# A two-block float32 transformer on one core: PSUM banks planned with the order of the products, eleven direct pairs turned into seven-product pairs, one weight sum made by an adding transfer, and a longer split ending

## The chip, the cores and the metric

One core of one Trainium2 chip runs the kernel. The metric is device microseconds of one execution, lower is better. Durations in the text come from one profiled execution of the kernel; its matmuls start one after the other and overlap in the pipeline, so the cost of one is the distance between starts, not its printed length.

## The reference

Two models run one after the other on a sequence of 512 tokens with 1024 features. The first has two layers of attention, retention, pooling and a convolutional MLP. The second puts 16 learned tokens ahead (528 tokens) and has two layers of gated MLP, mixer, gated MLP. The change touches only the second model's four gated MLPs and its end:

```python
def swiglu(x, w_gate, w_up, w_down):
    return (jax.nn.silu(x @ w_gate) * (x @ w_up)) @ w_down

for l in range(DEPTH):                                   # DEPTH = 2
    h = h + 0.5 * swiglu(rmsnorm(h, g[l, 0]), gate[l, 0], up[l, 0], down[l, 0])
    h = h + mixer(rmsnorm(h, g[l, 1]), ...)
    h = h + 0.5 * swiglu(rmsnorm(h, g[l, 2]), gate[l, 1], up[l, 1], down[l, 1])
return rmsnorm(h, final_norm)[:, 16:]
```

The width inside the MLP is 2816, so gate and up have 22 column blocks of 128 each. The last of the four MLPs needs only the 512 real tokens; the other three work on 528.

## The kernel before, in words

Activations lie transposed in SBUF: eight tiles `xt` of 128 features by 528 tokens. Every float32 operand is kept as a high part and a low part (`wsplit` L225, `split`, `xsplit`): ScalarE writes the rounded high part (`whi`, L226), VectorE the difference (`wlo`, L227), and TensorE adds three matmuls per block, high by high, high by low, low by high. So each weight tile of 128 x 512 costs one DMA on SP's queue, one ScalarE and one VectorE instruction.

`ffn2` (L1175) runs one gated MLP. Its 22 pairs (one block of gate, one of up) are done in three rounds that end at pairs 8, 16 and 22 (`ROUNDS`); after each round the down projection adds that round's activations into `xt`. A pair can be done in two ways:

- **direct** (`whole`, L1071): the gate block and then the up block, each with 8 k-steps of three matmuls over all tokens. With 528 tokens a matmul is cut in two (256 and 272 columns), so the pair has 96 matmuls; with 512 tokens it has 48 of 512 columns. It needs four weight parts.
- **seven products** (`strassen`, L1089): gate and up are seen as a 2 x 2 matrix of half blocks a, b (gate) and c, d (up), the tokens as two halves, and a Winograd form needs seven products instead of eight. A product has 4 k-steps of three matmuls over half the tokens, 12 matmuls, so the pair has 84. It needs seven weight parts: a, b, d and four sums of weights, made on VectorE in `parts_of` (L1031, the sums at L1049), and four sums of activations per k, made once per MLP by `form` (L340).

The names in the trace: `gu` is the PSUM tile of a direct block; `y`, `x`, `z` are those of the seven products. Y takes p1, p6, p7, p4 one on top of the other and ScalarE copies it out after each (L1104, L1113, L1121, L1126); X takes p2; Z takes p5 and p3; VectorE adds X and Z in (L1098). `act` (L1204) multiplies by the norm's factor, applies Silu, multiplies gate by up and splits.

What sets the order: `product_order` (L1136) writes the order of a round's products by hand, with a latency LAT of 24 matmuls (two products) between a product and one that needs its copy, and with three PSUM tiles to hold. TensorE keeps that order; SP's loads, the sums and the splits keep theirs (`queue`); the rest is placed by the framework's scheduler. A product's weights are split LEAD = 6 products ahead in the program; the buffers of raw, sum, high and low tiles are in `WB`. PSUM has a pool P of three tiles of two banks and a pool S of two banks; before, Y and Z come from P and X from S.

Some pairs are direct by a list, `DIRECT`: pairs 3, 12 and 18 in the first MLP, where three pairs come from work started ahead, and 0, 1, 5, 12 and 18 in the other three, where pairs 0 and 1 cover the wait for the norm's factor `rb`. At that entry (L1228 on) three blocks are multiplied before `rb` is known; then for each of the two pairs ahead the missing block is multiplied, some `form`s are made, the gate block is read out of PSUM by `mul_r` (VectorE, L447) and `act` follows. Three of the four forms of an MLP are made earlier, in `finish` (L331) of the stage ahead.

`ending` (L1281) closes the kernel: the last output block of the last down projection is done in two halves of 256 tokens, and each half has its chain: add to `xt`, square, sum (`compact`, tile `ssq`), `rsqrt` in ten small VectorE instructions, broadcast through TensorE (`bc`), eight multiplications in `finals` (L1305, tile `fy`) and eight output DMAs.

Of the kernel before, what the change touches and what calls it, by code (L numbers as in the profile page):

```python
# [49 lines left out]
WB = {1024: {"raw": 3, "whi": 5, "wlo": 5}, 512: {"raw": 6, "sum": 4, "whi": 8, "wlo": 8}}  # L50
# [11 lines left out]
class Net:  # L62
    def __init__(self, ctx, tc, d):
# [16 lines left out]
        self.forms = None  # L80
        self.pinned = False
# [135 lines left out]
    def wtile(self, n):  # L217
        dt = F32 if n in ("raw", "sum") else F32R
        return self.wp.tile([128, self.wu], dt, tag=n, name=self.nm(n), bufs=WB[self.wu][n])
# [111 lines left out]
    def finish(self, k, T, g):  # L331
# [4 lines left out]
        if self.forms is not None and NK // 2 <= k < NK - 1:  # L336
            self.form(k - NK // 2, T, g)
        return r

    def form(self, k, T, g):  # L340
# [7 lines left out]
        stt = lambda o, i, s, j: nc.vector.scalar_tensor_tensor(  # L348
            out=o, in0=i, scalar=s, in1=j, op0=ALU.mult, op1=ALU.subtract
        )  # L350
# [680 lines left out]
    def parts_of(self, gsrc, usrc):  # L1031


        nc = self.nc
        t = {}

        def get(n):
            if n in t:
                return t[n]
            if n in "abcd":  # L1040
                h = slice(512 * (n in "bd"), 512 * (n in "bd") + 512)
                t[n] = self.wtile("raw")
                self.queue("raw", nc.sync.dma_start(t[n], (gsrc if n in "ab" else usrc)[:, h]))
            else:
                i, j = {"s1": "cd", "s2": ("s1", "a"), "s3": "ac", "s4": ("b", "s2")}[n]
                i, j = get(i), get(j)
# [12 lines left out]
        return parts  # L1059
# [11 lines left out]
    def whole(self, i, xs, T, rb, act):  # L1071
# [3 lines left out]
        def one(o):  # L1075
            def go(w):
# [985 lines left out]
```

## Time and profile before

| | us |
|---|---|
| three runs, median (lowest to highest) | 3576.71 (3575.93 to 3577.52) |
| the profiled execution, its own time | 3577.7 |
| its span, first to last instruction | 3575.9 |
| TensorE busy | 3501.3 (98%), 23291 matmuls |
| VectorE busy | 2437.5 (68%) |
| ScalarE busy | 1718.5 (48%) |
| GpSimd busy | 44.3 (1%) |
| mean granted TensorE clock | 0.991 |
| DMA | 304.94 MB, mean 85 GB/s |

The four MLPs with their down projections stand at about 1236 to 1612, 2051 to 2418, 2418 to 2795 and 3205 to 3557 us of the span. A timeline row reads: start, length, engine, line, operation, output<-inputs, shape, count, and in brackets the engine's idle time ahead and what ended it.

### The profile page before, as it was taken

To read this page: it belongs to the slowest core of one execution; us is meant where nothing else is said; L and a number is where in the kernel's file an instruction comes from. 1 tells how busy PE (TensorE), PEld (TensorE's weight loads), DVE (VectorE), ACT (ScalarE), POOL (GpSimd) and SP (SyncE) were. 2 spreads that over 40 slices of the span, in tenths; PEclk is the share of its full clock that TensorE was granted. 3 is DMA by queue.
4 is the path that set the end of the run, shared out by engine and by line. 5 is a ranking of instruction groups with operands and counts; after the bars stand their busy time and mean duration, and the time that the engine had idled before them with its cause. 6 is when DMAs were issued, how large, how long until landed. Compare 5 with 4: busy or idle time off the path is not lost.

```text
span 3575.9 us, 59662 instructions
## 1 busy us (share of the span) xinstructions
PE 3501.3 (98%) x23291; PEld 3123.4 (87%) x23291; DVE 2437.5 (68%) x4715; ACT 1718.5 (48%) x3151; POOL 44.3 (1%) x184
## 2 busy tenths in 40 slices
PE   8999999999999999999999999999999999999998
PEld 6778888778888899998898999998999987788987
DVE  6778753776874387676545777678677764677767
ACT  3654432365543364354574454454444457545443
POOL 1000000000000000000000000000000000000000
PEclk9999999999999999999999999999999999999999
DMA  4213323212333232331111222332333212223232
GB/s 151 65 48 109 97 89 107 81 60 67 99 95 93 70 105 89 95 107 61 55 61 57 83 92 92 94 102 77 96 107 93 76 54 64 65 85 105 92 104 71
DMA packets 142954, 304.94 MB, mean 85 GB/s; under 512 B 16436, under 2 KB 24660, under 8 KB 142672
## 3 DMA queue, kind: packets, MB, share of 16 engines
q1 hardware_dynamic: 138672, 292.88, 26.1%
q0 software_dynamic: 2560, 6.93, 0.6%
q8 instruction: 183, 3.00, 0.3%
q10 hardware_dynamic: 1440, 1.32, 0.1%
q14 instruction: 99, 0.81, 0.1%
HBM read 298.97 MB, written 2.10 MB: 84 GB/s over the span
## 4 chain that ended last, share of the span: by engine, by line
PE 73%; DVE 5%; ACT 2%; issue 1%; DMA 0%; DVEq 0%; ACTq 0%
PE dn L241 15%; PE g L241 12%; PE y L241 11%; PE up L241 7%; PE gu L241 6%; PE z L241 5%; PE wo L241 3%; PE x L241 3%; PE pa L241 1%; PE pb L241 1%; PE oa L1531 1%; PE sc L1497 1%; DVE wlo L227 1%; PE go L1761 1%; PE ptr L1514 1%
## 5 line engine op out<-in xcount | busy, mean ns | idle before, releaser
L226 ACT ACTIVATE whi<-raw 128x512 fp32r<-128x512 f32 (+3 forms) x880 | 620.0, 708 | 879.2 <-PE dn L241 340.5
L227 DVE TENSOR_TENSOR wlo<-raw,whi 128x512 fp32r<-128x512 f32 (+3 forms) x880 | 687.8, 783 | 401.2 <-ACT whi L226 386.9
L241 PE MATMUL g<-xh,whi 128*128 128x256 f32 (+4 forms) x1192 | 330.4, 333 | 10.0 <-ACT xh L315 5.7
L241 PE MATMUL g<-xl,whi 128*128 128x256 f32 (+4 forms) x1192 | 317.9, 320 | 0.1
L241 PE MATMUL g<-xh,wlo 128*128 128x256 f32 (+4 forms) x1192 | 316.1, 320 | 0.0
L241 PE MATMUL up<-xl,whi 128*128 128x512 f32 (+1 forms) x768 | 288.7, 376 | 0.1
L241 PE MATMUL up<-xh,wlo 128*128 128x512 f32 (+1 forms) x768 | 288.6, 376 | 0.0
L241 PE MATMUL up<-xh,whi 128*128 128x512 f32 (+1 forms) x768 | 287.9, 376 | 0.0
L241 PE MATMUL dn<-fah,whi 128*128 128x256 f32 (+1 forms) x1238 | 286.4, 300 | 1.2 <-ACT fah L235 0.6
L241 PE MATMUL dn<-fah,wlo 128*128 128x256 f32 (+1 forms) x1238 | 285.3, 299 | 0.0
L241 PE MATMUL dn<-fal,whi 128*128 128x256 f32 (+1 forms) x1238 | 285.1, 299 | 0.0
L226 ACT ACTIVATE whi<-sum 128x512 fp32r<-128x512 f32 x268 | 169.2, 632 | 219.0 <-PE dn L241 72.4
L241 PEld LDWEIGHTS g<-xh,whi 128*128 128x128 f32 (+1 forms) x1192 | 198.0, 188 | 46.1 <-issue 18.1
L227 DVE TENSOR_TENSOR wlo<-sum,whi 128x512 fp32r<-128x512 f32 x268 | 184.2, 687 | 47.9 <-ACT whi L226 43.7
L241 PEld LDWEIGHTS g<-xh,wlo 128*128 128x128 f32 (+1 forms) x1192 | 200.3, 188 | 15.4
L241 PEld LDWEIGHTS g<-xl,whi 128*128 128x128 f32 (+1 forms) x1192 | 200.7, 189 | 14.1 <-issue 1.6
L241 PEld LDWEIGHTS dn<-fah,whi 128*128 128x128 f32 x1238 | 199.8, 188 | 10.8 <-ACT fah L235 3.9
L241 PEld LDWEIGHTS dn<-fal,whi 128*128 128x128 f32 x1238 | 199.4, 188 | 7.9 <-DVE fal L236 0.8
L241 PEld LDWEIGHTS dn<-fah,wlo 128*128 128x128 f32 x1238 | 199.7, 188 | 7.3
L241 PEld LDWEIGHTS up<-xl,whi 128*128 128x128 f32 x768 | 145.1, 189 | 28.3 <-DVE xl L316 0.5
L241 PEld LDWEIGHTS up<-xh,wlo 128*128 128x128 f32 x768 | 145.2, 189 | 28.0
L241 PEld LDWEIGHTS up<-xh,whi 128*128 128x128 f32 x768 | 144.7, 189 | 27.5
(503 smaller groups left out, 8704.0 us busy)
## 6 DMA issues: line engine op xcount, KB each, us to landing
raw<-w_up SPq DMA_DIRECT2D x88, 512.0 KB, 3.6
raw<-ffn_g SPq DMA_DIRECT2D x176, 256.0 KB, 2.6
raw<-ffn_u SPq DMA_DIRECT2D x176, 256.0 KB, 2.9
raw<-ffn_d SPq DMA_DIRECT2D x160, 256.0 KB, 2.7
raw<-w_in SPq DMA_DIRECT2D x136, 256.0 KB, 2.6
raw<-w_down SPq DMA_DIRECT2D x32, 512.0 KB, 3.5
raw<-w_in SPq DMA_DIRECT2D x25, 512.0 KB, 3.6
raw<-w_out SPq DMA_DIRECT2D x16, 512.0 KB, 3.5
```

The source lines that it names most:

```text
L226: h = self.nc.scalar.activation(hi[:, c], raw[:, c], AF.Copy)
L227: l = self.nc.vector.tensor_tensor(out=lo[:, c], in0=raw[:, c], in1=hi[:, c], op=ALU.subtract)
L241: i = self.nc.tensor.matmul(*a, **k)
L1497: nc.tensor.matmul(o, lhsT=q, rhs=kk[:, kc], start=i == 0, stop=i == len(ops) - 1)
L1514: nc.tensor.transpose(tr[:, 128 * b : 128 * b + 128], p[:, 128 * b : 128 * b + 128], self.ident)
L1531: nc.tensor.matmul(o[a], lhsT=lh, rhs=rh, start=b == 0, stop=b == 4)
L1761: nc.tensor.matmul(o(b), lhsT=lh, rhs=rh, start=i == 0, stop=i == len(terms) - 1)
```

## The change

Seven edits in one diff. (1) `DIRECT` loses pairs 12 and 18 in the first MLP and 5, 12 and 18 in the other three: eleven pairs by this diff become seven-product pairs. (2) `product_order` now plans the two PSUM pools by themselves and returns which pool each product takes: p1 from P or S, p2 and p5 from S or P. (3) The Winograd form is rewritten with other signs, so that all weight sums are sums: t1 = c+d, t2 = t1+a, t3 = t2+b, t4 = a+c; one product is negated in `form` and one factor in `act`. (4) t4 is not made on VectorE any more: SP loads a into a tile `acc` (two buffers) and a DMA on GpSimd's queue adds c to it. High and low weight buffers go from 8 to 7. (5) Raw loads are issued AHEAD = 5 products before their splits. (6) At the entry of the three MLPs, `act` comes before the forms, and two forms instead of three are made in the stage ahead. (7) `ending` does the last two output blocks in halves, with the second half's second PSUM tile from S; the factor is copied to SBUF, and both halves' final multiplications come after both chains in the program.

```diff
-WB = {..., 512: {"raw": 6, "sum": 4, "whi": 8, "wlo": 8}}
+WB = {..., 512: {"raw": 6, "sum": 4, "acc": 2, "whi": 7, "wlo": 7}}
 LEAD = 6
-USES = {"p1": ("a",), "p2": ("b",), "p6": ("s2",), "p5": ("s1",), "p7": ("s3",), "p4": ("d",), "p3": ("s4",), "g": "ab", "u": "cd"}
+AHEAD = 5
+USES = {"p1": ("a",), "p2": ("b",), "p6": ("t2",), "p5": ("t1",), "p7": ("t4",), "p4": ("d",), "p3": ("t3",), "g": "ab", "u": "cd"}
-DIRECT = (0, 1, 5, 12, 18), (3, 12, 18)
+DIRECT = (0, 1), (3,)
...
-        if self.forms is not None and NK // 2 <= k < NK - 1:
+        if self.forms is not None and NK // 2 <= k < NK // 2 + self.early:
...
-        nc.scalar.activation(t[:, a], x1[:, a], AF.Copy, scale=g1)
-        stt(u[:, a], x1[:, b], g1, t[:, a])
-        stt(v[:, a], x2[:, b], g2, u[:, a])
-        nc.vector.tensor_tensor(out=u[:, b], in0=v[:, a], in1=t[:, a], op=ALU.subtract)
+        nc.scalar.activation(t[:, a], x1[:, b], AF.Copy, scale=g1)
+        stt(u[:, a], x1[:, a], g1, t[:, a])
+        stt(u[:, b], x2[:, b], g2, t[:, a])
+        stt(v[:, a], x1[:, a], g1, u[:, b], ALU.add)
         stt(v[:, b], x2[:, a], g2, v[:, a])
-        self.forms.append((self.split(u[:, :T], "fu"), self.split(v[:, :T], "fv")))
+        h, l = self.slot("fvh", F32R), self.slot("fvl", F32R)
+        nc.scalar.activation(h[:, :T], v[:, :T], AF.Copy, scale=-1.0)
+        stt(l[:, :T], v[:, :T], -1.0, h[:, :T])
+        self.forms.append((self.split(u[:, :T], "fu"), (h, l)))
...
+        of = {"t1": "cd", "t2": ("t1", "a"), "t3": ("t2", "b")}
+
+        def ahead(n):
+            if n in of:
+                for x in of[n]:
+                    ahead(x)
+            elif n not in t:
+                t[n] = self.wtile("acc" if n == "t4" else "raw")
+                self.queue("raw", nc.sync.dma_start(t[n], src["a" if n == "t4" else n]))
+                if n == "t4":
+                    nc.gpsimd.dma_start(t[n], src["c"], accum_op=ALU.add)
...
-                op = ALU.add if n == "s1" else ALU.subtract
-                self.queue("sum", nc.vector.tensor_tensor(out=t[n], in0=i, in1=j, op=op))
+                self.queue("sum", nc.vector.tensor_tensor(out=t[n], in0=i, in1=j, op=ALU.add))
...
+        bank = lambda kd, n: self.P(n)[:, 0, :h] if kd == "P" else self.S(n)[:, :h]
-            Y = ps["Y"] = self.P("y")[:, 0, :h]
+            Y = ps["Y"] = bank(kd, "y")
-            X = self.S("x")[:, :h]
+            X = bank(kd, "x")
-            Z = ps["Z"] = self.P("z")[:, 0, :h]
+            Z = ps["Z"] = bank(kd, "z")
...
-        takes, frees = {"p1", "p5", "g", "u"}, {"p4", "p3", "g", "u"}
+        takes = {"p1": "PS", "p5": "SP", "p2": "SP", "g": "P", "u": "P"}
+        frees = {"p4": "p1", "p3": "p5", "p2": "p2", "g": "g", "u": "u"}
-        hold = []
+        pool, has = {"P": [0] * 3, "S": [0] * 2}, {}
...
                 if o in takes:
-                    busy = [f for f in hold if f is None or f > t]
...
+                    at, _, kd = min((max(at, min(pool[q])), j, q) for j, q in enumerate(takes[o]))
+                    if at >= inf:
+                        continue
...
-            nc.vector.tensor_tensor(out=s[:, :T], in0=s[:, :T], in1=u, op=ALU.mult)
+            if scale:
+                nc.vector.scalar_tensor_tensor(out=s[:, :T], in0=u, scalar=-1.0, in1=s[:, :T], op0=ALU.mult, op1=ALU.mult)
...
+                gt = ps[0] if o == 4 else self.mul_r(ps[0], rb, "fg")
+                if not done:
+                    act(o // 2, gt, ps[1], False)
                 forms(1 + (o == 0) - (o == 4))
-                gt = ps[0] if o == 4 else self.mul_r(ps[0], rb, "fg")
-                act(o // 2, gt, ps[1], False)
+                if done:
+                    act(o // 2, gt, ps[1], False)
...
-            for n in range(len(order) + LEAD):
-                if n < len(order):
-                    i, o = order[n]
+            for n in range(-AHEAD, len(order) + LEAD):
+                if n + AHEAD < len(order):
+                    i, o, _ = order[n + AHEAD]
                     if i not in get:
                         get[i] = self.parts_of(srcs[2 * ms[i]], srcs[2 * ms[i] + 1])
-                    w[i, o] = [get[i](p) for p in USES[o]]
+                    if o == "p7":
+                        get[i][1]("t4")
+                if 0 <= n < len(order):
+                    i, o, _ = order[n]
+                    w[i, o] = [get[i][0](p) for p in USES[o]]
...
-                self.forms = self.next_forms
+                self.forms, self.early = self.next_forms, 2
...
-                self.ending(out, self.wload(dsrc(NK - 1)), acts, rb)
+                self.ending(out, [self.wload(dsrc(i)) for i in (NK - 2, NK - 1)], acts, rb)
...
-        ps = [self.outs(1, NX, "dn")[0][0] for _ in range(2)]
+        ps = [[self.outs(1, NX, "dn")[0][0] for _ in ws], [self.outs(1, NX, "dn")[0][0], self.S("dl")]]
...
+            for m, p, w in zip((NK - 2, NK - 1), ps[hf], ws):
...
             self.bcast(self.rsqrt(pss, bl, 1), bl, bc)
-            self.finals(out, bc, c)
+            rb = self.slot("rbe")
+            nc.scalar.copy(rb[:, c], bc[:, c])
+            bcs.append((rb, c))
+        for rb, c in bcs:
+            self.finals(out, rb, c)
```

## Rows read from the trace of the kernel before

**Rows 1.** The page: busy time of TensorE, its share and instructions.

```profile
PE 3501.3 (98%) x23291; PEld 3123.4 (87%) x23291; DVE 2437.5 (68%) x4715; ACT 1718.5 (48%) x3151; POOL 44.3 (1%) x184
```

**Rows 2.** Busy time by stretch, in the third MLP: a run of products, and an entry.

```profile
core 0: us, PE busy (x) PEld busy (x) DVE busy (x) ACT busy (x) POOL busy (x), PEclk, DMA share, GB/s
2565.56:2603.56 38.00, 38.00 (x315) 38.00 (x313) 32.14 (x55) 22.71 (x45) 0.00 (x0) 1.00 0.37 119
...
2446.00:2447.40 1.40, 1.40 (x6) 1.40 (x7) 1.15 (x2) 0.63 (x2) 0.00 (x0) 0.50 0.00 0
```

**Rows 3.** Timeline of TensorE: first matmuls of stretches, with 528 and with 512 tokens.

```profile
2565.56 0.28 PE L241 MATMUL y<-xh,whi 128*128 128x264 f32 x1
...
2603.56 0.41 PE L241 MATMUL gu<-xh,whi 128*128 128x256 f32 x2
...
2609.41 0.28 PE L241 MATMUL y<-fvh,whi 128*128 128x264 f32 x1
...
3254.58 0.39 PE L241 MATMUL gu<-xh,whi 128*128 128x512 f32 x1
...
3260.12 0.28 PE L241 MATMUL y<-fuh,whi 128*128 128x256 f32 x1
...
3261.54 0.39 PE L241 MATMUL gu<-xh,whi 128*128 128x512 f32 x1
```

**Rows 4.** The page: splits of summed weights, all four MLPs.

```profile
L227 DVE TENSOR_TENSOR wlo<-sum,whi 128x512 fp32r<-128x512 f32 x268 | 184.2, 687 | 47.9 <-ACT whi L226 43.7
```

**Rows 5.** Timeline of VectorE inside that run of products.

```profile
2585.41 0.70 DVE L236 TENSOR_TENSOR fal<-fg,fah 128x528 fp32r<-128x528 f32 x1
2586.03 0.43 DVE L1098 TENSOR_TENSOR fu<-z,fu 128x264 f32<-128x264 f32 x1
...
2586.71 0.68 DVE L227 TENSOR_TENSOR wlo<-raw,whi 128x512 fp32r<-128x512 f32 x1
2587.31 0.68 DVE L227 TENSOR_TENSOR wlo<-sum,whi 128x512 fp32r<-128x512 f32 x1
```

**Rows 6.** Tile y: what TensorE sat idle for ahead of its matmuls (us, times).

```profile
  ACT fg L1104: 4.6, 4
```

**Rows 7.** Timeline of TensorE at the entry of the third MLP.

```profile
2424.34 0.48 PE L241 MATMUL gu<-xh,whi 128*128 128x256 f32 x2 [1.73 <-DVE fd L1269]
...
2431.34 0.49 PE L241 MATMUL gu<-xh,whi 128*128 128x256 f32 x2 [0.90 <-DVE fd L1269]
...
2445.99 0.78 PE L241 MATMUL gu<-xh,whi 128*128 128x256 f32 x2 [4.37 <-DVE fg L447]
...
2454.10 0.28 PE L241 MATMUL y<-xh,whi 128*128 128x264 f32 x1
```

**Rows 8.** Timeline of ScalarE and VectorE at the same entry.

```profile
2438.72 0.66 ACT L441 COPY rbc<-bc 128x512 f32<-128x512 f32 x2 [5.48 <-PE bc L418]
...
2445.15 0.70 DVE L447 TENSOR_TENSOR fg<-gu,rbc 128x528 f32<-128x528 f32 x1
```

**Rows 9.** DMA issues: count, KB each, median us from issue to landing.

```profile
raw<-ffn_g SPq DMA_DIRECT2D x176, 256.0 KB, 2.6
...
ropc<-rope_ax POOLq DMA_DIRECT2D x2, 264.0 KB, 3.2
...
sda<-rope_da POOLq DMA_DIRECT2D x2, 256.0 KB, 5.9
```

**Rows 10.** Timeline of ScalarE: first copy of Y in that run of products.

```profile
2567.68 0.36 ACT L1104 COPY fg<-y 128x264 f32<-128x264 f32 x1
```

**Rows 11.** Timeline of TensorE and VectorE after the last down projection.

```profile
3556.33 0.28 PE L241 MATMUL dn<-fah,wlo 128*128 128x256 f32 x1
...
3560.34 3.22 DVE L1310 SCALAR_TENSOR_TENSOR fy<-xt,v,bc 128x256 f32<-128x256 f32 x8 [0.81 <-PE bc L418]
3563.48 0.41 DVE L1294 SCALAR_TENSOR_TENSOR fd<-dn,rbc 128x256 f32<-128x256 f32 x1
...
3569.75 3.22 DVE L1310 SCALAR_TENSOR_TENSOR fy<-xt,v,bc 128x256 f32<-128x256 f32 x8 [1.38 <-PE bc L418]
```

More of the change, by code (lines that the diff above doesn't have):

```diff
@@ L80, in __init__ @@
         self.forms = None
+        self.early = 3
         self.pinned = False
@@ L217, in wtile @@
     def wtile(self, n):
-        dt = F32 if n in ("raw", "sum") else F32R
+        dt = F32 if n in ("raw", "sum", "acc") else F32R
         return self.wp.tile([128, self.wu], dt, tag=n, name=self.nm(n), bufs=WB[self.wu][n])
@@ L1035, in parts_of @@
         t = {}
-        def get(n):
[L1038 to L1046, printed above, removed]
+        src = {n: (gsrc if n in "ab" else usrc)[:, 512 * (n in "bd") : 512 * (n in "bd") + 512] for n in "abcd"}
+        of = {"t1": "cd", "t2": ("t1", "a"), "t3": ("t2", "b")}
[8 more added lines that the diff above has]
+                    nc.gpsimd.dma_start(t[n], src["c"], accum_op=ALU.add)
+        def get(n):
+            ahead(n)
+            if n not in t:
+                i, j = (get(x) for x in of[n])
                 t[n] = self.wtile("sum")
-                op = ALU.add if n == "s1" else ALU.subtract
-                self.queue("sum", nc.vector.tensor_tensor(out=t[n], in0=i, in1=j, op=op))
+                self.queue("sum", nc.vector.tensor_tensor(out=t[n], in0=i, in1=j, op=ALU.add))
             return t[n]
@@ L1057, in parts @@
             return h, l
-        return parts
+        return parts, ahead
     def prod(self, o, w, xs, c, first):
@@ L1150, in product_order @@
                     break
-                at = max([t] + [end[m, d] + (0 if (d, o) in (("p1", "p2"), ("p1", "p5"), ("p5", "p7")) else LAT) for d in need.get(o, ()) if (m, d) in end])
                 if any((m, d) not in end for d in need.get(o, ())):
                     continue
+                at = max([t] + [end[m, d] + (0 if (d, o) in (("p1", "p2"), ("p1", "p5"), ("p5", "p7")) else LAT) for d in need.get(o, ())])
+                kd = None
                 if o in takes:
-                    busy = [f for f in hold if f is None or f > t]
-                    if len(busy) >= 3:
-                        if None in busy and sum(f is None for f in busy) >= 3:
-                            continue
-                        at = max(at, sorted(f for f in busy if f is not None)[len(busy) - 3])
+                    at, _, kd = min((max(at, min(pool[q])), j, q) for j, q in enumerate(takes[o]))
+                    if at >= inf:
+                        continue
                 if best is None or at < best[0]:
-                    best = (at, m, o)
-            at, m, o = best
+                    best = (at, m, o, kd)
+            at, m, o, kd = best
             t = at + (48 if o in ("g", "u") else 12)
@@ L1165, in product_order @@
             left.remove((m, o))
-            if o in takes:
-                hold = [f for f in hold if f is None or f > at]
-                hold.append(t + LAT if o in ("g", "u") else None)
-            elif o in frees:
-                hold.remove(None)
-                hold.append(t + LAT)
-            out.append((m, o))
+            if kd:
+                j = pool[kd].index(min(pool[kd]))
+                pool[kd][j] = inf
+                has[m, o] = kd, j
+            if o in frees:
+                q, j = has[m, frees[o]]
+                pool[q][j] = t + LAT
+            out.append((m, o, kd))
         return out
@@ L1261, in ffn2 @@
             if fin:
-                self.forms = self.next_forms
+                self.forms, self.early = self.next_forms, 2
             dsrc = lambda i: dw[i][:, 128 * m0 : 128 * m1]
-            for i in range(NK - 1 if fin and out is not None else NK):
+            for i in range(NK - 2 if fin and out is not None else NK):
                 p = self.outs(1, T, "dn")[0]
@@ L1288, in ending @@
             bl = (2 * hf, 2 * hf + 1)
-            n = len(acts)
-            for k in range(n):
-                self.mm3(ps[hf], ws, 128 * k, acts[k], NX, k == 0, k == n - 1, halves=(hf,))
-            xv = self.xt[m][:, c]
-            t = self.slot("fd")
-            nc.vector.scalar_tensor_tensor(
-                out=t[:, c], in0=ps[hf][:, c], scalar=0.5, in1=rf[:, c], op0=ALU.mult, op1=ALU.mult
-            )
-            nc.vector.tensor_tensor(out=xv, in0=t[:, c], in1=xv, op=ALU.add)
-            self.sumsq(m, xv, c)
+            for m, p, w in zip((NK - 2, NK - 1), ps[hf], ws):
+                for k in range(n):
+                    self.mm3(p, w, 128 * k, acts[k], NX, k == 0, k == n - 1, halves=(hf,))
+                xv = self.xt[m][:, c]
+                t = self.slot("fd")
+                nc.vector.scalar_tensor_tensor(
+                    out=t[:, c], in0=p[:, c], scalar=0.5, in1=rf[:, c], op0=ALU.mult, op1=ALU.mult
+                )
+                nc.vector.tensor_tensor(out=xv, in0=t[:, c], in1=xv, op=ALU.add)
+                self.sumsq(m, xv, c)
             pss = self.S("ssq")
```

32 lines of the change are left out of this document (18 added, 14 removed).

## The prediction, made before the changed kernel was run

> **What bounds the kernel.** I read the page first: TensorE is busy 98% of the span [rows 1], so a saving counts only if it takes matmuls off TensorE or ends one of its few waits. Next the busy time by stretch: in a run of 26 products TensorE is busy 38.00 of 38.00 us at full granted clock, VectorE 32.14 and ScalarE 22.71, GpSimd nothing [rows 2]. So the MLPs are bound by TensorE, VectorE is the next in line, and GpSimd's queue is free. Then the timeline for the pace of each kind of work [rows 3], and last the places where TensorE sits idle [rows 6, 7] and the tail, where it has nothing left to do [rows 11].
>
> **Eleven direct pairs become seven products.** By the diff the lists lose 2 pairs in the first MLP and 3 in each of the other three: 8 with 528 tokens, 3 with 512 (I count eleven). With 528 tokens the 26 products from 2565.56 to 2603.56 take 38.00 us, 1.462 each, and the half of a direct pair that follows takes 2609.41 - 2603.56 = 5.85 [rows 3]. A pair costs 2 x 5.85 = 11.70 direct and 7 x 1.462 = 10.23 in products: 1.47 saved. With 512 tokens a half takes 5.54 and a product 1.42 [rows 3]: 11.08 against 9.94, 1.14 saved. Sum: 8 x 1.47 + 3 x 1.14 = **15.2 us**, all on the path, since TensorE has no gap there.
>
> **Does VectorE keep up?** The 268 splits of sums are four for each of 67 pairs [rows 4]. On VectorE a split or a sum of 512 columns takes 0.60 from start to start, a pass over all tokens 0.62, over half of them 0.34 [rows 5]. Per pair before: 7 splits, 4 sums, 3 halves and 3 whole passes, 11 x 0.60 + 3 x 0.34 + 3 x 0.62 = 9.5 us beside 10.23 of TensorE (93%). Without the fourth sum: 8.9 (87%). So the relief by the direct pairs is not needed any more: a round of only products asks less of VectorE per microsecond than a stretch of products does now, and that runs without a gap [rows 2]. Three splits more on ScalarE for each pair, and the negation (other signs and a product in one pass of the same kind), cost nothing: ScalarE is 60% busy there [rows 2].
>
> **The adding transfer.** It replaces a sum by an SP load of a, then a GpSimd DMA that waits for it and adds c; the trace has no adding DMA. Bounds: the load 2.6 us, GpSimd's plain loads between 3.2 and 5.9 [rows 9], so 5.8 to 8.5 us together; I take 6 to 7, near the 3.2 row, which is the load issued beside the MLP's work. It is issued 5 products ahead of its split, 5 x 1.462 = 7.3 us, and the split itself is up to 6 products ahead of the matmuls. Behind the split on ScalarE waits the copy of Y; such a copy ended at 2567.68 + 0.36 = 2568.04, 1.0 us after its product (2565.56 + 1.462 = 2567.02) [rows 3, 10], and has two products, 2.9 us, until p6. So up to 7.3 + 1.9 = 9.2 us stay hidden: cost 0. SP's queue issues one load more per pair and GpSimd's two norm tables come after the last adding DMA; both queues have idle time around that. Only a page has a price for what VectorE can do to such a DMA: the Trainium skill, "SBUF — State Buffer", section "SBUF: two separate sides", says that descriptors of GpSimd's DMAs are written by its cores, which are locked out while VectorE runs an instruction in a two-port mode, and its next section gives 620 ns turned into 3100. By it, as an estimate, 2.5 us come on top of the bounds above and the upper one no longer fits; the VectorE rows of this stretch show 512 columns in 0.60 us and no faster form [rows 5], which speaks against it here.
>
> **PSUM by plan.** Z moves from P to S beside X, so S's two tiles turn over faster: p5 of a pair follows p2's reader by two products, 2.9 us. VectorE reads X directly after its product unless it is late by more than that. Cost 0 up to there. Weight buffers 8 to 7 take one product off a lead of seven; cost 0 for the same reason as above.
>
> **Waits inside rounds.** TensorE waits four times, 4.6 us together, for the first copy of a late pair's Y [rows 6], once in each MLP's first round, when the direct pair there lets VectorE's and ScalarE's work bunch up behind it. Three of those direct pairs go (the first MLP keeps pair 3). Bounds: all three waits go (3.5) or new ones of that size come (3.5 lost), since a form more has to fit in there; I take **1.9 gained**.
>
> **The entry of the third MLP.** The fourth block waits 4.37 us for `mul_r` to free PSUM, and its matmuls then run slowly: from 2445.99 to 2454.10 are 8.11 us where 5.85 is the pace, and the granted clock is 0.50 of full, the lower of the two levels, after that idle time [rows 2, 7]. So the wait costs 4.37 + 2.26 = 6.6. The factor was there at 2438.72 + 0.66 = 2439.4, but a form and splits stood ahead of `mul_r` until 2445.15 [rows 8]. With `act` ahead, `mul_r` comes at about 2440, before the three blocks end (2445.99 - 4.37 = 2441.6). One form fewer in the down projection takes off the wait of 0.90, not that of 1.73, which is behind the second form [rows 7]. Against it: two forms, 2 x (4 x 0.40 + 2 x 0.62) = 5.7 us of VectorE by those rates, must end before p5; I leave 1.5 us for that. Bounds 0 to 7.5, taken: **6.0 gained**. At the second and fourth MLP no such wait shows, and the form moved there costs 0 to 1.5, inside the bound of the waits above.
>
> **The ending.** TensorE's last matmul starts at 3556.33 and the span ends at 3575.9: 19.4 us. The second half's chain starts at 3563.48, behind the eight `fy` of the first half [rows 11]. In the changed kernel the second half's last block ends about where it did (72 matmuls of 256 columns at 0.118 for 18 of 512 and 36 of 256, +0.1). Chain: 0.3, then 3563.48 to 3569.75 = 6.27, the new copy 0.5, eight `fy` 3.22, and 3575.9 - 3572.97 = 2.93 for the output: 13.2 if the first half's `fy` fit into the chain's pauses, 16.4 if none does. Gain 2.9 to 6.1; **4.5** taken.
>
> **Sum.** 15.2 + 1.9 + 6.0 + 4.5 = 27.6. Against the profiled execution's own 3577.7 that is 3550.1; the median of the runs is 1.0 lower, so 3549.
>
> **Rivals.**
> - *The products are saved, the rest is not*: new waits eat what the entry and the ending give. For it: VectorE at 87% for eight pairs on end, S shared by X and Z, and the forms later. Against it: the gapless runs at 93%. Then 3577 - 15 = 3562, or 3570 and no measurable change if TensorE waits 0.1 us more in each of 78 pairs. Chance 0.10 for a clear gain of that size, 0.05 for none.
> - *The adding transfer is late*, the slower side: place, ScalarE's split of t4, with the copies of Y behind it. Price: each microsecond past the hidden 9.2 is paid by each of 78 pairs. It takes back the 27.6 from 9.2 + 27.6 / 78 = 9.6 us on; at 10 us the kernel takes 3549 + 0.8 x 78 = 3611. For it: the slowest GpSimd load gives 8.5 and adding may take longer than writing; against it: the near row gives 5.8, and SP can issue earlier than the program's 7.3. Chance 0.05. The lock of that page of the Trainium skill would act in this place: as an estimate, 8.3 us by the near row, still hidden, and 11.0 by the far one.
> - *The change does not do what it says*: the scheduler puts the first half's `fy` ahead of the second chain again, and the forms ahead of `act`. Then 3577 - 15 - 2 = 3560; inside the first rival's chance.
>
> **Chances.** A measurement of this kernel can tell about 0.2%, 7 us, from no change. Forecast 0.80 and the milder first rival 0.10 are faster, 0.05 is the same, 0.05 slower. Range: below, all bounds at their best, 15.2 + 3.5 + 7.5 + 6.1 = 32.3, and the 1.73 wait too, 34: 3543; above, the products alone: 3562.
>
> **What would show it.** the eleven pairs' matmuls are 924 where they were 912 (768 of 256 or 272 columns and 144 of 512, now 672 of 264 and 252 of 256); 234 sums on VectorE where 268 were, for 78 pairs; product runs still at 1.462; TensorE's idle time ahead of y gone but for one of 1.1; no idle time of 4 us at the third entry and full clock behind it; `fy` of both halves after both chains, the tail near 15 us. I am wrong if t4's split on ScalarE waits for a DMA, if tile x or z gets idle time ahead of it, or if VectorE runs full in the second rounds.

## The result: slower by 1%, and the profile after

The changed kernel takes 3614.15 us (median of 4, 3612.22 to 3616.39) against 3577.05 for the kernel before (4 runs, 3575.93 to 3577.52): ratio 1.0104, interval 1.0090 to 1.0118. The forecast was 3549, so it missed by 65 us and by its sign.

The page of the changed kernel, against [rows 1]:

```profile
span 3610.4 us, 60204 instructions
...
PE 3500.0 (97%) x23321; PEld 3126.3 (87%) x23321; DVE 2444.2 (68%) x4750; ACT 1748.3 (48%) x3231; POOL 111.7 (3%) x262
```

TensorE's busy time hardly fell although 11 pairs now take 84 matmuls each. Part of the 15 us saved went into matmuls at half clock (the mean granted clock is 0.987 where it was 0.991), and the span grew by waits. Tile y shows them, against the 4.6 us of [rows 6]:

```profile
  ACT fu L1134: 51.0, 37
  ACT fg L1117: 24.2, 8
```

L1117 is the copy of Y after p1, L1134 the one after p7. The rows count weight loads beside matmuls, so a wait stands in them more than once; from the starts of matmuls I get 16 waits ahead of p4, 25.8 us, and 12.6 us in four waits ahead of p6 (before: none, and 5.2 us in four). A third place is new, p5 waiting for a form, 13.7 us in three rounds. The timeline of TensorE at the second MLP's first round shows both it and the wait ahead of p6:

```profile
2087.23 0.39 PE L243 MATMUL z<-fuh,whi 128*128 128x264 f32 x1 [2.75 <-ACT fuh L237]
...
2088.82 0.59 PE L243 MATMUL z<-ful,whi 128*128 128x264 f32 x1 [1.20 <-DVE ful L238]
...
2092.46 0.59 PE L243 MATMUL y<-fvh,whi 128*128 128x264 f32 x1 [2.83 <-ACT fg L1117]
```

The stretches behind it (columns: us, busy time and count of TensorE, weight loads, VectorE, ScalarE, GpSimd, then granted clock, DMA share, GB/s):

```profile
2080.30:2087.23 6.93, 4.18 (x35) 3.98 (x33) 6.55 (x13) 4.55 (x8) 0.86 (x1) 1.00 0.51 129
2087.23:2092.46 5.23, 1.20 (x3) 0.69 (x3) 3.75 (x7) 2.07 (x4) 0.00 (x0) 0.57 0.34 80
2092.46:2098.00 5.54, 5.54 (x25) 5.54 (x26) 1.46 (x3) 0.93 (x3) 0.00 (x0) 0.50 0.00 0
2098.00:2102.50 4.50, 4.50 (x38) 4.50 (x38) 2.56 (x5) 2.40 (x5) 0.07 (x1) 0.98 0.40 136
...
2235.00:2273.00 38.00, 37.61 (x309) 37.40 (x308) 33.15 (x59) 23.57 (x48) 2.58 (x3) 1.00 0.54 148
```

After the waits the granted clock is 0.50, the lower level, and 25 matmuls take 5.54 us, 0.222 each where the pace is 0.122. The last row answers to [rows 2]: VectorE is busy 33.15 of 38.00 us, the 87% that was forecast; it isn't full.

The second kind of wait, ahead of p4, comes in every round, once at the same place (12 of the 16; the other four come two pairs later). TensorE at that place in a second round, then ScalarE there:

```profile
2223.23 0.29 PE L243 MATMUL x<-xh,wlo 128*128 128x264 f32 x1
2225.20 0.39 PE L243 MATMUL y<-fvh,whi 128*128 128x264 f32 x1 [1.68 <-ACT fu L1134]
```

```profile
2221.89 0.65 ACT L1223 ACTIVATE fg<-fg 128x528 f32<-128x528 f32 x1 [0.77 <-DVE fg L1222]
2222.45 0.62 ACT L228 ACTIVATE whi<-acc 128x512 fp32r<-128x512 f32 x1
2223.72 0.64 ACT L237 ACTIVATE fah<-fg 128x528 fp32r<-128x528 f32 x1 [0.65 <-DVE fg L1226]
2224.27 0.61 ACT L228 ACTIVATE whi<-raw 128x512 fp32r<-128x512 f32 x1
2224.79 0.36 ACT L1134 COPY fu<-y 128x264 f32<-128x264 f32 x1
```

The copy (L1134) stands on ScalarE's queue behind Silu (L1223) and the split (L237) of the pair before, and each of these waits for VectorE. p3 of that pair ends right ahead of p7, whose copy this is.

Where the 34.5 us between the spans came from, by the first and last product matmul of each round in TensorE's timeline (us; for the kernel before the rounds hold its direct pairs; the other columns are experiments below, each with the edits of the column to its left but for the last, which has an entry and an ending of its own; other work is what is left of the span):

| stretch | before | changed | p5 back | + 3 forms | + AHEAD 0 | best |
|---|---|---|---|---|---|---|
| first round, first MLP | 44.5 | 49.9 | 47.8 | 47.8 | 44.7 | 45.0 |
| first rounds, other three MLPs | 196.3 | 226.9 | 218.8 | 194.1 | 194.9 | 191.0 |
| the other eight rounds | 591.0 | 604.2 | 584.9 | 586.6 | 584.7 | 582.7 |
| last product of MLP 2 to first of MLP 3 | 70.6 | 63.6 | 63.7 | 63.8 | 63.8 | 63.8 |
| last product to end of span | 52.1 | 52.7 | 49.7 | 51.2 | 50.3 | 49.2 |
| other work | 2621.4 | 2613.1 | 2615.8 | 2614.9 | 2614.2 | 2617.8 |
| span | 3575.9 | 3610.4 | 3580.7 | 3558.4 | 3552.6 | 3549.5 |

### The profile page after: what moved, and what is told of

Read it like the earlier page. It is cut to its first block, busy times and chain, and to the rows that moved or that the text cites. A ratio compares the mean times of both kernels' runs of the same rounds, so it can differ in the third digit from the quotient of the medians.

```text
span 3610.4 us, 60204 instructions
## 1 busy us (share of the span) xinstructions
PE 3500.0 (97%) x23321; PEld 3126.3 (87%) x23321; DVE 2444.2 (68%) x4750; ACT 1748.3 (48%) x3231; POOL 111.7 (3%) x262
## 4 chain that ended last, share of the span: by engine, by line
PE 71%; DVE 5%; ACT 3%; DMA 1%; issue 1%; SPq 0%; DVEq 0%; ACTq 0%
PE dn L243 16%; PE g L243 12%; PE y L243 11%; PE up L243 7%; PE z L243 5%; PE wo L243 3%; PE x L243 3%; PE gu L243 2%; DMA raw<-ffn_u 1%; PE pa L243 1%; PE pb L243 1%; PE oa L1564 1%; PE sc L1530 1%; PE go L1794 1%; DVE wlo L229 1%
## 5 line engine op out<-in xcount | busy, mean ns | idle before, releaser
L228 ACT ACTIVATE whi<-sum 128x512 fp32r<-128x512 f32 x234 | 147.5, 631 | 184.2 <-PE y L243 81.4
L243 PE MATMUL y<-fvh,whi 128*128 128x264 f32 (+1 forms) x624 | 182.9, 293 | 34.8 <-ACT fu L1134 23.2
L243 PEld LDWEIGHTS g<-xh,wlo 128*128 128x128 f32 (+1 forms) x1192 | 199.4, 188 | 15.2
L229 DVE TENSOR_TENSOR wlo<-sum,whi 128x512 fp32r<-128x512 f32 x234 | 160.5, 687 | 52.2 <-ACT whi L228 49.5
L243 PE MATMUL y<-fvh,wlo 128*128 128x264 f32 (+1 forms) x624 | 179.0, 287 | 0.0
L243 PE MATMUL y<-fvl,whi 128*128 128x264 f32 (+1 forms) x624 | 178.8, 287 | 0.0
```

What stands on the lines that cost most here:

```text
L228: h = self.nc.scalar.activation(hi[:, c], raw[:, c], AF.Copy)
L229: l = self.nc.vector.tensor_tensor(out=lo[:, c], in0=raw[:, c], in1=hi[:, c], op=ALU.subtract)
L243: i = self.nc.tensor.matmul(*a, **k)
```

## The experiments

Times are medians; ratios are to the kernel before, run beside each.

**The saved products alone.** The kernel before with `DIRECT = (0, 1), (3,)`.

> The kernel before with the shorter lists of direct pairs and nothing else. This measures the first term by itself: 11 pairs as products, 15.2 us by the pace of the product runs. If the term stands: 3560 to 3564. Rival (the direct pairs let VectorE and ScalarE catch up, and four sums per pair don't keep up without them): less than 7 us gained, 3570 or more, with new waits of TensorE ahead of y.

3561.18 us, ratio 0.9954 (0.9939 to 0.9969): 15.6 us saved against 15.2 forecast. The term stands, and four sums per pair keep up without the direct pairs, nearly: three of the four waits ahead of p6 go (5.2 us become 1.2), and 3.5 us ahead of p4 come, in four places. The first rounds of the other three MLPs take 188.5 us here and the other eight rounds 588.8; the changed kernel's 226.9 and 604.2 are to be held against these, since both have the same pairs as products.

**The order of the products.** First the whole old planner in the changed kernel, with the places of p1, p5 and p2 in PSUM that go with it:

```diff
...
-            out.append((m, o, kd))
+            out.append((m, o, {"p1": "P", "p5": "P", "p2": "S"}.get(o)))
```

> The changed kernel with the order of products and the places in PSUM as before (p1 and p5 from P, p2 from S, at most three of P held); all else as changed, the adding transfer too. Theory O (the order 'p4 p3 of one pair, then p7 of the next' leaves one product, 1.46 us, for VectorE and ScalarE to finish act before the copy of Y that p4 needs): with p5 in between again the waits for the copy of Y after p7 go: 25 to 35 us less, about 3584. Rival T (the transfer): they stay, within 7 us of 3614.

3578.96 (10 runs, 3570.39 to 3583.33), ratio 1.0002 (0.9992 to 1.0011): 35 us back, all that was expected. Run on their own, the two planners give lists that differ in one place of each round: the new one lets p5 of the second pair take its bank in S before p4 and p3 of the first have run. Then only that place:

```diff
+        for j in range(len(out) - 3):
+            m = out[j][0]
+            if [x[:2] for x in out[j : j + 4]] == [(m, "p5"), (m - 1, "p4"), (m - 1, "p3"), (m, "p7")]:
+                out[j : j + 3] = out[j + 1 : j + 3] + out[j : j + 1]
```

> The changed kernel with one product moved: the two planners' orders differ in one place of each round of five, six or eight pairs, where the changed one has p5 of the next pair ahead of p4 and p3 of the pair before, so that p3 stands directly ahead of p7. Here p5 goes back between p3 and p7, once per round; Z stays in S, all else as changed. (This place is passed once in each of the 12 rounds, and there TensorE waits for the copy of Y, 16 waits of 25.8 us in all with those that follow; the 45 given for the run without the adding transfer counted matmuls of several products.) Theory O: as the run with the whole old planner, 3574 to 3582. Rival P (what cost was Z in S beside X, two tiles for both, and the old planner helped by its places): nearer to 3614 than to 3579.

3583.05 (10 runs, 3575.76 to 3584.87), ratio 1.0015 (1.0006 to 1.0025). One product moved once per round is worth 31 us, 1 us short of the range expected; theory O holds. This run and the one before it have the same order and differ in the places in PSUM alone, so Z in S costs the 4 us between them at most, less than either spreads. Tile y in this kernel:

```profile
  ACT fg L1117: 24.0, 8
...
  ACT fu L1134: 3.6, 7
```

The wait ahead of p4 is gone but for 1.5 us in two places, the ones ahead of p6 (12.5 us) and p5 (12.5) stay: two causes. ScalarE at the place where the changed kernel waited:

```profile
2212.99 0.65 ACT L1227 ACTIVATE fg<-fg 128x528 f32<-128x528 f32 x1
2213.89 0.64 ACT L228 ACTIVATE whi<-raw 128x512 fp32r<-128x512 f32 x1 [0.26 <-PE y L243]
2215.08 0.65 ACT L237 ACTIVATE fah<-fg 128x528 fp32r<-128x528 f32 x1 [0.55 <-DVE fg L1230]
...
2216.15 0.36 ACT L1134 COPY fu<-y 128x264 f32<-128x264 f32 x1
```

Silu, split and copy follow each other as before, but p5 now stands between p3 and p7, so TensorE asks for the copy one product, 1.46 us, later.

**The forms.** First the whole entry as before (forms ahead of `mul_r` and `act`, three forms in the down projection), in the changed kernel and in the one with p5 back:

```diff
+                forms(1 + (o == 0) - (o == 4))
                 gt = ps[0] if o == 4 else self.mul_r(ps[0], rb, "fg")
-                if not done:
-                    act(o // 2, gt, ps[1], False)
-                forms(1 + (o == 0) - (o == 4))
-                if done:
-                    act(o // 2, gt, ps[1], False)
+                act(o // 2, gt, ps[1], False)
...
-                self.forms, self.early = self.next_forms, 2
+                self.forms, self.early = self.next_forms, 3
```

> The changed kernel with the entry of the MLPs as before: each form stands ahead of mul_r and act again, and the down projection makes three forms ahead instead of two. All else as changed. Theory A (late forms): in the changed kernel TensorE waits at the start of the first round of MLPs 2, 3 and 4 for the last form (2.75 us for fuh, 1.20 for ful, 2.83 for the copy of Y at 2087 to 2092, and the like at 2473 and 3257), with the granted clock at 0.50 for some 10 us behind it; the product runs of these rounds take 12 to 14 us more than their products. With the forms early these waits go, 3 x 11 = 33 us, and the wait of 4.4 us at the third entry with its slow clock, 6.6 us, comes back: 26 us less, about 3588. Rival (the waits at the start of a round come from the products' order or the weights, not the forms): the time stays within 7 us of 3614.

> The same with the entry of before as well (forms ahead of mul_r and act, three forms in the down projection). If theory A (late forms, TensorE waits 5.9 us for p5 of the first pair in three first rounds, and the clock is at 0.50 behind it) and theory O stand side by side, the two savings add up: 3579 less 26 for the first rounds, plus 6 for the wait of mul_r at the third entry, which is in the 26 already: 3551 to 3558. If the late forms and the order share one cause (VectorE's and ScalarE's backlog), the second saving is less than 10 us: 3569 or more.

3597.01 (ratio 1.0054, 1.0039 to 1.0069) and 3567.00 (0.9971, 0.9960 to 0.9981). Alone the edit gives 17 us, not 26, between its two expectations; behind the order it gives 16, not 25 to 32, and misses both of its ranges. In the second, the three first rounds fall from 218.8 to 187.9 us, more than expected; the third entry takes back 6.5, the ending 2.7 (a matter of clock, below), other stages 2.7: 19 us between the two profiled executions. Which half of the entry's edit does it? With p5 back, only the number of forms:

```diff
-                self.forms, self.early = self.next_forms, 2
+                self.forms, self.early = self.next_forms, 3
```

> The changed kernel with one product put back (3583) and three forms in the down projection instead of two; act still ahead of the last form. Which half of the entry's edit made the forms late? If the number of forms left (two behind act): the three first rounds, 73.2, 73.6 and 72.0 us, fall to 64 to 66, the time by 20 or more, to 3563 or less. If act ahead of any form (the last form waits for act's chain however few are left): they stay at 69 or more, 3571 or above.

3562.97, ratio 0.9958 (0.9944 to 0.9971): 20 us from one number, as the first expectation had it. The number of forms left is the cause. `act` ahead of the last form does less: against the whole old entry 6.2 us are left in the three first rounds (194.1 and 187.9), about what the third entry gives back. VectorE in the changed kernel, with its two forms (L350) among splits, and the second one's end:

```profile
2079.04 0.89 DVE L350 SCALAR_TENSOR_TENSOR tu<-xt,v,tt 128x264 f32<-128x264 f32 x2
...
2081.70 0.71 DVE L350 SCALAR_TENSOR_TENSOR fvl<-tv,fvh 128x528 fp32r<-128x528 f32 x1
...
2083.55 0.89 DVE L350 SCALAR_TENSOR_TENSOR tu<-xt,v,tt 128x264 f32<-128x264 f32 x2
...
2086.85 0.70 DVE L350 SCALAR_TENSOR_TENSOR fvl<-tv,fvh 128x528 fp32r<-128x528 f32 x1
...
2088.07 0.70 DVE L238 TENSOR_TENSOR ful<-tu,fuh 128x528 fp32r<-128x528 f32 x1
```

p1 starts at 2080.30 and p5 two products later, 2083.2; the second form ends at 2088.77. With one form left (stretches of that kernel, from the round's start) the clock stays at 1.00, and one wait is left:

```profile
2075.49:2082.00 6.51, 4.86 (x40) 4.65 (x39) 6.17 (x11) 5.04 (x9) 0.86 (x1) 1.00 0.57 160
2082.00:2090.00 8.00, 8.00 (x68) 8.00 (x67) 5.51 (x11) 4.12 (x9) 0.70 (x1) 1.00 0.50 130
```

```profile
2081.67 0.39 PE L243 MATMUL y<-fvh,whi 128*128 128x264 f32 x1 [1.66 <-ACT fg L1117]
```

**The adding transfer.** t4 as a fourth sum (`of = {..., "t4": "ac"}`, no `acc` tile, no DMA on GpSimd), in the changed kernel and, later, in a repaired one:

> The changed kernel with t4 = a + c made by VectorE as a fourth sum from the loaded weights; no adding transfer, no load of a second a, no acc tiles; all else as changed (order, direct lists, entry, ending, seven split buffers). In the changed kernel TensorE waits 1.1 to 2.3 us for the copy of Y after p7, 45 times, in all rounds. Theory T (the transfer or its place in SP's queue makes the weights late, so that VectorE and ScalarE run late): these waits go, 25 to 35 us less, about 3584. Rival O (the order of the products brings act of one pair too close to p7 of the next): the waits stay, the time stays within 7 us of 3614, or rises by some us since VectorE has 0.6 us more per pair.

> The best version so far (changed kernel with one product put back, forms early, mul_r ahead, new ending: 3557) with t4 = a + c as a fourth sum by VectorE in place of the adding transfer. With the order right, what does the transfer give or take? Its split starts 12.4 us or more after the transfer's issue, and the slowest landed in 5.9, so it is never waited for. Theory (the transfer is hidden, and the sum it saves was hidden too): within 4 us of 3557. Rival (VectorE needs the relief): 3561 or more. Rival (the transfer holds SP's queue or buffers): 3553 or less.

3603.06 (1.0071, 1.0056 to 1.0086) in the first, 11 us less, of which 3 are in the ending: between the two theories, and the waits ahead of p4 stay, 18.1 us. 3564.63 (0.9964, 0.9951 to 0.9976) in the second, 7 us more than with the transfer, as its first rival said (the other eight rounds 597.2 us against 586.7): in that kernel the sum that the transfer saves is worth something. That it is so in general is not shown: with `AHEAD` left at 5 the edit also loads c earlier, and the kernel with four sums at the end of this section comes within 2 us of the best with the transfer. The transfers of the changed kernel, issue and landing (the second row takes SP's loads into `acc` and the adding DMAs together; the adding DMAs alone land in 3.6 to 5.9 us, median 4.4):

```profile
L1054 POOL DMA_DIRECT2D acc<-ffn_u x78: 848/860/899, 1264.7 to 3528.7; - x78
...
DMA to landing us min/median/max: 2.5/3.7/5.9
```

The earliest split of t4 starts 12.8 us after GpSimd's issue, so no transfer is late for its own split.

**The transfer five products ahead.** Point (5) of the change has raw loads issued five products early; by the diff only t4's are, the load into `acc` and the adding DMA, while a, b, c and d keep their places. `AHEAD = 0` takes that away, first in a repaired kernel, then alone in the changed one, then with the two small edits above.

> The best version so far (3557) with AHEAD = 0: loads and the adding transfer are issued where the splits are, not five products ahead. Without them the transfer has the splits' own lead of six products, 8.8 us, less the time that the loads wait for buffers. If the program's place decides: the transfer (3.5 us from SP's load to GpSimd's issue and 4.4 to land) comes late in some pairs, ScalarE's split waits for it, and the time rises by 5 us or more. If the queues issue by buffers anyway: within 3 us of 3557, and the first round of the first MLP (45.7 us, 44.6 in the kernel before with the lists) may lose 1 us since the sums no longer stand ahead of its forms.

> The changed kernel (3614) with AHEAD = 0 and nothing else. In the best version this edit took 6.5 us off. If the early loads are a cause of their own: 3605 to 3611, and the once-per-round wait for the copy of Y (1.4 to 2.3 us, 12 rounds) and the waits for the forms stay. If the wait for the copy of Y comes from sums and splits that the early loads let in ahead of act on VectorE: 3590 or less, and those waits fall below 1 us.

> The changed kernel with three small edits: p5 one place later once per round, three forms in the down projection, AHEAD = 0. act ahead of the last form, the ending, the adding transfer, signs, lists and PSUM places as changed. If the three are the whole loss against the forecast: 3563 (measured with the first two) less 5 to 7 = 3556 to 3558, and the rest to 3551 is act's place (3 to 4 us in the first rounds) and the ending (2 to 3). If the early loads only hurt where act stands behind the form: 3561 or more.

3550.77 (0.9924, 0.9911 to 0.9938), 3593.56 (1.0046, 1.0031 to 1.0061) and 3556.48 (0.9943, 0.9926 to 0.9960). Six to seven us behind the other edits, 21 alone. The first met neither of its two expectations, since it got faster; the alone run falls between its two; the third lies in its range. In the alone run the waits ahead of p4 stay once per round, but at 1.1 to 1.4 us instead of 1.4 to 2.3, and the other four go: 14.1 us instead of 25.8. The transfer still isn't late: its split starts 8.7 us after the issue or more. What it does is slow the loads beside it. SP's and GpSimd's queues of the changed kernel in the second round, ahead of the wait shown (the two `ffn_u` loads are c and d of a later pair):

```profile
2211.99 0.33 SPq L1052 DMA_DIRECT2D acc<-ffn_g  x1
2212.41 0.38 SPq L1052 DMA_DIRECT2D raw<-ffn_g  x1
2213.08 3.28 SPq L1052 DMA_DIRECT2D raw<-ffn_u  x2
...
2215.07 0.86 POOL L1054 DMA_DIRECT2D acc<-ffn_u  x1 [6.63 <-DVE fu L1110]
```

The same two loads with `AHEAD = 0` alone (this round starts 4.37 us earlier), and the load of t4, now behind them:

```profile
2208.71 3.28 SPq L1052 DMA_DIRECT2D raw<-ffn_u  x2
2212.08 0.38 SPq L1052 DMA_DIRECT2D acc<-ffn_g  x1
```

Counted from the round's start, c is issued at 10.25 us and d at 13.21 in both. But d takes 3.45 us to land where the adding transfer is under way beside it, and 2.58 without. It is so in all 12 rounds: this load takes 2.9 to 3.8 us in the changed kernel, always beside an adding transfer, and 2.4 to 2.9 with `AHEAD = 0`, never beside one. Over all of them, the changed kernel and then `AHEAD = 0` alone:

```profile
raw<-ffn_u SPq DMA_DIRECT2D x176, 256.0 KB, 3.3
...
raw<-ffn_u SPq DMA_DIRECT2D x176, 256.0 KB, 2.7
```

VectorE of the changed kernel waits for d to make t1, with the norm's factor (L1222) of the pair before queued behind; in the other run the sum starts without a wait:

```profile
2219.61 0.69 DVE L1061 TENSOR_TENSOR sum<-raw,raw 128x512 f32<-128x512 f32 x1 [0.64 <-DMA raw<-ffn_u]
2220.22 0.42 DVE L1110 TENSOR_TENSOR fg<-z,fg 128x264 f32<-128x264 f32 x1
2220.56 0.68 DVE L229 TENSOR_TENSOR wlo<-sum,whi 128x512 fp32r<-128x512 f32 x1
2221.16 0.70 DVE L1222 TENSOR_TENSOR fg<-fg,rbc 128x528 f32<-128x528 f32 x1
```

```profile
2214.47 0.68 DVE L1061 TENSOR_TENSOR sum<-raw,raw 128x512 f32<-128x512 f32 x1
```

The sum starts 0.77 us earlier in its round there, and TensorE's wait ahead of p4 is shorter by the same 0.77 us (1.08 instead of 1.85, from the starts of matmuls). This also fits the smaller gain behind the order: p5 between p3 and p7 covers one product, 1.46 us, of the same wait, and with p5 back only 1.5 us of the 25.8 are left. Half of what the edit gives there is in the first MLP's first round (47.8 to 44.7 us).

**The ending.** All four half blocks' matmuls ahead of the first chain, in the changed kernel (the lines taken out of the loop below are left out):

```diff
+        for hf in range(2):
+            for p, w in zip(ps[hf], ws):
+                for k in range(n):
+                    self.mm3(p, w, 128 * k, acts[k], NX, k == 0, k == n - 1, halves=(hf,))
```

> The changed kernel with one edit in the ending: the matmuls of all four half blocks stand ahead of the first half's chain, so that bc of the first half can't stand ahead of dl on TensorE. In the changed kernel TensorE waits 1.84 us for rsqrt before bc, and the 18 matmuls of dl behind it run at 0.213 us instead of 0.118. Theory: the time from the last dn block to the end shrinks by 2.9 us of idle time and 1.7 us of slow clock, and the whole by 4 to 5: about 3610. Rival (the end is set by VectorE's fy behind both chains, whatever TensorE does): within 1.5 us of 3614.

3619.98 (1.0118, 1.0101 to 1.0134). It meets neither expectation. TensorE's last matmul starts 5.4 us earlier behind the last product, but the stretch from there to the end shrinks only from 52.7 to 51.0 us, 1.7 and not 4 to 5: the first half's chain now starts behind all matmuls, 2.0 us later. The whole is slower by 6: the rounds, which the edit doesn't touch, took 7.6 us more in the profiled execution (49.9 to 51.7, 226.9 to 227.2 and 604.2 to 609.7). Why is not shown.

**Versions that beat both.** The changed kernel with p5 back, three forms, `mul_r`, form and `act` in this order, and an ending whose second half's matmuls stand between ssq and rsqrt of the first; with `AHEAD = 0` it is the run above, the best column of the table, 3550.77. And the kernel before with lists, `mul_r` ahead of the form and the same ending:

```diff
+                gt = ps[0] if o == 4 else self.mul_r(ps[0], rb, "fg")
                 forms(1 + (o == 0) - (o == 4))
-                gt = ps[0] if o == 4 else self.mul_r(ps[0], rb, "fg")
```

The ending of both, where `mms(1)` stands for the matmuls of the second half's two blocks:

```diff
             self.compact(self.acc, bl, self.c1024, pss)
+            if hf == 0:
+                mms(1)
+            else:
+                self.finals(out, *bcs[0], range(3))
             bc = self.S("bc")
             self.bcast(self.rsqrt(pss, bl, 1), bl, bc)
+            if hf:
+                self.finals(out, *bcs[0], range(3, NK))
```

> The changed kernel with the order of one product put back, with mul_r ahead of the form and the form ahead of act at the entry, three forms in the down projection, and another ending: the second half's matmuls stand between the first half's ssq and its rsqrt, and the first half's fy stand partly in the second chain's pauses. If late forms, order and ending are the whole loss: 3579 less 26 in the first rounds, less 5 at the third entry, less 3 to 5 at the end: 3543 to 3550, faster than both. Rival (the mul_r ahead makes the form late again): first rounds still 3 us or more over their products each, 3553 or more.

> The kernel before with three things only: the shorter lists of direct pairs, mul_r ahead of the form at the entry of the MLPs (form still ahead of act), and the ending that the best version so far uses. Four sums per pair, signs, order of products, PSUM places, eight split buffers as before; no adding transfer. By stages: 3561 with the lists alone (measured), less 6 for the third entry (70 to 64 us between its rounds), less 3.5 for the end (51.7 to 48.2): 3551 to 3553. Rival (the version with the adding transfer and three sums, 3557, is worth something of its own, so that without it VectorE is late): 3557 or more.

3557.29 (0.9949, 0.9932 to 0.9966) and 3552.20 (0.9928, 0.9914 to 0.9941). The first misses its range: its first rounds are where they should be, 191.7 us, and what was left was the early transfer, 6.5 us by `AHEAD = 0`. The second lies in its range, so most of the gain needs neither the transfer nor the new planner.

## Why the prediction was wrong

The products' gain was right. Three costs that the prediction put at nothing or nearly so are the loss: the new order of products (PSUM by plan), the form moved into the first rounds, and the early transfer. Undoing these three brings back 58 of the 65 us. The gain at the end failed as well.

- **Eleven pairs as products, 15.2 gained: right**, 15.6 alone. VectorE's 87% was met, though the step's 93% for the stretch of [rows 2] was not: that row has 32.14 of 38.00 us, 85%, at the start of a round and ahead of a direct pair. With the lists alone and four sums it is 34.24 of 38.00 in a second round, 90%.
- **The entry of the third MLP, 6.0 gained: right for the wait of 4.37 us** ([rows 7]): 70.6 to 63.6 us between the MLPs. **Wrong beside it**: the step said that two forms cost 1.5 us at most before p5 and that "At the second and fourth MLP no such wait shows, and the form moved there costs 0 to 1.5". It cost 8.2 us in each of three MLPs (218.8 to 194.1). The step summed the two forms' own work, 5.7 us, but VectorE runs them among splits and sums, from 2079.04 to 2088.77, 9.7 us; the second ended 5.6 us after p5's turn, and the clock that fell with it was paid too, as it had been in [rows 7], where I had counted it. One form left instead of two takes the wait ahead of p5 away.
- **PSUM by plan, cost 0: wrong, 31 us.** The step looked at banks only and never wrote down the two orders side by side. They differ in one place per round, and that place puts p3 right ahead of p7, so that TensorE waits for the copy of Y ahead of p4: 25.8 us, and 1.5 with p5 back.
- **The adding transfer, cost 0: right in its own term**, since it is never late: SP to GpSimd 3.5 us and 4.4 to land (medians), 7.9 together, lie in the bounds of 5.8 to 8.5, and 12.1 us or more lie between issue and split in the eight runs with the transfer ahead. **Wrong in what it left out**: it counted the idle time of the two queues and not what the transfer does to loads beside it. Five products ahead it falls on the loads of c and d, which are needed sooner, and d takes 0.4 to 1.3 us longer to land; this is 6 to 7 us behind the other repairs and 21 alone. The lock that the Trainium skill gives ("SBUF — State Buffer", "SBUF: two separate sides") isn't seen: all 78 issues on GpSimd took 0.85 to 0.90 us, and the slowest landed in 5.9, like the slower row of [rows 9].
- **Waits inside rounds, 1.9 gained: wrong.** It treated the one place in the first rounds and no other. There its better bound came true with the lists alone, 5.2 us of waits to 1.2; in the changed kernel they grew to 12.6, and with the old entry and p5 back one is left, 4.1, in the first MLP.
- **The ending, 4.5 gained: lost 0.6.** The tail behind TensorE's last matmul was right, 15.3 us with bounds of 13.2 to 16.4 (its start value, 19.4, should read 19.6: 3575.9 less 3556.33). The step that failed took it that the last block ends about where it did: it starts its last matmul 37.4 us behind the last product and not 32.6. TensorE waits for the first half's rsqrt with `dl` queued behind, and `dl` then runs at 0.213 us instead of 0.118:

```profile
3588.43 0.28 PE L243 MATMUL dn<-fah,wlo 128*128 128x256 f32 x1
3590.39 1.22 PE L423 MATMUL bc<-cst,rs_y 128*128 128x128 f32 x4 [1.68 <-DVE rs_y L409]
3591.27 0.56 PE L243 MATMUL dl<-fah,whi 128*128 128x256 f32 x1
3591.63 0.41 PE L243 MATMUL dl<-fal,whi 128*128 128x256 f32 x1
3591.84 0.41 PE L243 MATMUL dl<-fah,wlo 128*128 128x256 f32 x1
```

With these matmuls between ssq and rsqrt instead, the last of them starts after 32.9 us and the stretch takes 48.2 to 49.2, 2.9 to 3.9 gained.

Of the signs named, "tile x or z gets idle time" came true for z; t4's split never waited and VectorE wasn't full. The slower side was given to the transfer alone, and to its being late, which it wasn't; the order and the loads beside the transfer had no rival of their own, and the forms stood only among the reasons for a rival that kept the products' gain. With three small edits the changed kernel stands at 3556.48, with a better ending and entry at 3550.77, beside the forecast of 3549: the gains were there, and the rest of the change took them away more than twice over. What stays open: the three losses work on the same backlog of VectorE and ScalarE (31, 21 and 17 us alone, 58 together), and how they share it is shown for the wait ahead of p4 alone. The edit that takes the transfer back moves SP's load and the adding DMA together, so which of the two slows the loads isn't shown by itself; in the rows above d was under way from 13.2 to 16.7 us of its round, the adding DMA from 12.2 to 16.0, and SP's load into `acc` had landed at 11.7.

## What to carry to other kernels

When a planner changes, write both orders down and compare them place by place; a product that moves by one place can cost more than eleven direct pairs gain. Work moved out of a stage with idle engines into a busy entry costs its time on the crowded engine, not its own length, and the clock behind it. A transfer issued earlier than needed can be paid by the loads beside it, so compare their landing times and not only its own slack.

## What the runs showed of the hardware that was not expected

A load is slower beside an adding transfer. In the changed kernel the `ffn_u` loads of 256 KB that overlap an adding DMA by more than 1 us (108) land in 3.36 us in the median, those that overlap none (30) in 2.67; with `AHEAD = 0` alone it is 3.26 (40) and 2.64 (113).

The same wait of TensorE, 1.7 us ahead of `bc`, is followed by the lower clock in some executions and not in others (one execution of each kernel is profiled): `dl` starts every 0.213 us in the changed kernel above, at a granted clock of 0.50, and every 0.118, at 1.00, in the run with the entry as before, where the program of the ending is the same:

```profile
3573.26 0.71 PE L423 MATMUL bc<-cst,rs_y 128*128 128x128 f32 x4 [1.69 <-DVE rs_y L409]
3573.73 0.36 PE L243 MATMUL dl<-fah,whi 128*128 128x256 f32 x1
3573.93 0.28 PE L243 MATMUL dl<-fal,whi 128*128 128x256 f32 x1
3574.05 0.28 PE L243 MATMUL dl<-fah,wlo 128*128 128x256 f32 x1
```

It is worth 2 to 3 us of the end. Some of these kernels also spread more: the one with the old planner, which waits 5.9 us ahead of p5 in three first rounds, lies within 13 us in 10 runs, where the kernel before stays within 4 in 13. That the waits cause the spread is not shown.
